# Seven half-size products for the in-projection of a conv and mLSTM layer, with one stream of split weights

## The chip, the cores and the metric

The kernel runs on one core of one Trainium2 chip. The metric is the device time of one launch in microseconds. The kernel before takes 2620.36 us (median of three runs, 2616.11 to 2622.33). Its profile is of one execution with a span of 2622.1 us. Engine names are those of the profile: PE multiplies matrices, PEld loads its weights, DVE, ACT and POOL work on vectors, SP issues the transfers.

## The reference, cut to what matters

One layer works on 2176 tokens of 1024 features: 128 context tokens, then 2048 latent ones, all through the same weights, modulated apart. Everything is fp32.

```python
h = rmsnorm(x, norm1) * (1 + scale1) + shift1
z = h @ w_in                     # 1024 x 3600: conv b, c, x; q, k, v, o; 16 gate columns
y_sc = sc_b * conv3(sc_c * sc_x)                    # short gated convolution, 512 columns
h_m, C, n, m = mlstm_bidir(q, k, v, gates, C0, n0, m0)   # chunks of 128 tokens, both directions
h_m = headnorm(h_m) * sigmoid(o)
x = x + gate1 * (concat[y_sc, h_m] @ w_out)
h2 = rmsnorm(x, norm2) * (1 + scale2) + shift2
up = conv3(h2 @ w_up)                               # 2 x 2816 columns
x = x + gate2 * ((silu(g) * a) @ w_down)
```

The scales, shifts and gates come from `silu(c) @ w_mod`, 48 tiles of 128 values for two conditionings.

## The kernel before, in words

An fp32 product is made of three: every operand is split into a high part (a copy that is rounded to fp32r) and a low part (the difference), and high x high, high x low and low x high are summed in PSUM. A split costs a copy on ACT (`wh`, `hH`) and a subtraction on POOL or DVE (`wl`, `hL`).

Tokens are taken in six blocks: five of 384 and one of 256. The second half (blocks 3 to 5, list `BB`) comes first, then the first half (`BA`). `load_w` fetches a weight tile of 1024x128, copies it on ACT (L105) and subtracts in two pieces of 512 on POOL (L108). `gemm` (L196 to L198) multiplies one weight tile with one token block: 24 matmuls, eight feature tiles by three products. `vg` (L333 to L335) makes v and the gates with the tokens as the stationary operand, 24 matmuls of 264 columns for every chunk of 128 tokens and each of two halves of the columns. So the 24 weight tiles other than v are each loaded twice, once for a half of the tokens.

The stages, in order: 16 modulation tiles on PE with the loads behind them (to about 41 us); the second half through `vg`, `heads` and `shortconv` (to about 430 us), beside which DVE makes the other 32 modulation tiles (`mod_dve`, 64 dot products of 1024 at L499); `vg` of the first half and the rows of the gates (to 477 us); `Sums`, 34 units that go backwards over the chunks (about 490 to 690 us), and `Mix`, 34 units that make the outputs (to about 1015 us). `weave` puts one block of `gemm` between two stages of these units (`fill`: q, o, the conv and the out-projection of the first half, and blocks 2 and 3). The rest of the out-projection ends at 1106 us. Then the up projection (L938 to L940) from 1114 us and the down projection (L1030 to L1032) from 2066 us.

The up projection already uses seven half-size products in place of eight (Strassen-Winograd): weights in quarters, four extra additions on DVE for a pair of tiles (L269), seven splits (ACT at L275, subtractions at L276: three on POOL, four on DVE), and sums of tokens that are made once and stored (`sums`, L229 to L235).

Every engine works through its own list in program order, and waits at the head of the list for semaphores. SP issues almost all transfers in program order.

Of the kernel before, what the change touches and what calls it, by code (L numbers as in the profile page):

```python
# [18 lines left out]
P = 128  # L19
D = 1024  # L20
KT = 8
# [3 lines left out]
H = 4  # L25
# [9 lines left out]
BA = (0, 1, 2)  # L35
BB = (3, 4, 5)
# [6 lines left out]
def chunks(b):  # L43
    t0, n = BL[b]
    return range(t0 // P, (t0 + n) // P)
# [8 lines left out]
def hymba_kernel(ctx: ExitStack, tc: tile.TileContext, I, O):  # L54
# [17 lines left out]
    uD = dr.tile([FT, P, T], F32, name="uD")  # L72

# [20 lines left out]
    ssp = ctx.enter_context(tc.tile_pool(name="ssp", bufs=2))  # L94

# [4 lines left out]

    def load_w(src, n=1024):
        st = wp.tile([P, WN], F32, name="wst", bufs=2)
        Q.dma_start(st[:, :n], src)
        wh = wp.tile([P, WN], F32R, name="wh")
        S.activation(wh[:, :n], st[:, :n], AF.Copy)  # L105
        wl = wp.tile([P, WN], F32R, name="wl")
        for a in (0, n // 2):
            G.tensor_sub(wl[:, a:a + n // 2], st[:, a:a + n // 2], wh[:, a:a + n // 2].bitcast(F32))  # L108
        return wh, wl
# [18 lines left out]
    def spread(r, n):  # L128
        """PSUM [P, n]: the columns of r along the free dimension, on every partition."""
# [6 lines left out]
    def load_x(b, src, pool, name, bufs):  # L136
        t0, n = BL[b]
        xt = []
        for kh in range(2):
            x = pool.tile([P, 4, 384], F32, name=name, bufs=bufs)  # L140
            Q.dma_start(x[:, :, :n], src[4 * kh:4 * kh + 4, :, t0:t0 + n].rearrange("k p t -> p k t"))
            xt.append(x)
        return xt

    def rcol(b):
        t0, n = BL[b]
        return rc[:, t0 // P:(t0 + n) // P]

    def squares(b, xt):
        n = BL[b][1]  # L150
        ss = ssp.tile([P, 384], F32, name="ss")
        for k in range(KT):
            x = xt[k // 4][:, k % 4, :n]
            if k == 0:
                S.activation(ss[:, :n], x, AF.Square)
                continue
            sq = sqp.tile([P, 384], F32, name="sq")
            S.activation(sq[:, :n], x, AF.Square)
            V.tensor_add(ss[:, :n], ss[:, :n], sq[:, :n])
        return ss  # L160

    def apply(b, xt, norm):
        t0, n = BL[b]
        rb = spread(rcol(b), n)
        hH, hL = h_pair()
        sh = 0 if norm == 0 else 24
        for k in range(KT):
            x = xt[k // 4][:, k % 4]
            for a, e, v in spans(t0, t0 + n):
                a, e = a - t0, e - t0  # L170
                V.scalar_tensor_tensor(x[:, a:e], x[:, a:e], ab[:, norm, k, v:v + 1], rb[:, a:e],
                                       op0=ALU.mult, op1=ALU.mult)
                sv = modT[:, sh + k, v:v + 1]
                if k % 2 == 0:
                    S.activation(hH[:, k, a:e], x[:, a:e], AF.Identity, bias=sv)
                    V.scalar_tensor_tensor(hL[:, k, a:e], x[:, a:e], sv, hH[:, k, a:e].bitcast(F32),
                                           op0=ALU.add, op1=ALU.subtract)
                else:
                    S.activation(x[:, a:e], x[:, a:e], AF.Identity, bias=sv)
                    S.activation(hH[:, k, a:e], x[:, a:e], AF.Copy)  # L180
                    G.tensor_sub(hL[:, k, a:e], x[:, a:e], hH[:, k, a:e].bitcast(F32))
        return hH, hL

    def h_pair():
        pool = hps[next(turn) % 3]
        return [pool.tile([P, KT, 384], F32R, name=n) for n in ("hH", "hL")]

    def make_h(b, src, norm):
        return apply(b, load_x(b, src, xp, "xt", 2), norm)

    def gemm(w, h, n):
        (wh, wl), (hH, hL) = w, h
        acc = pa.tile([P, 512], F32, name="acc")
        for k in range(KT):
            w_h, w_l = wh[:, k * P:(k + 1) * P], wl[:, k * P:(k + 1) * P]
            PE.matmul(acc[:, :n], w_h, hH[:, k, :n], start=(k == 0), stop=False)  # L196
            PE.matmul(acc[:, :n], w_h, hL[:, k, :n], start=False, stop=False)  # L197
            PE.matmul(acc[:, :n], w_l, hH[:, k, :n], start=False, stop=(k == KT - 1))  # L198
        return acc
# [60 lines left out]
    def weights(j):  # L260
        """The split weights of the seven products."""
        st = fp.tile([P, 2, 1024], F32, name="st", bufs=2)
        for m in range(2):
            Q.dma_start(st[:, m], I["w_up"][m * FT + j])
        a11, a12, a21, a22 = (st[:, m, k:k + 512] for m in range(2) for k in (0, 512))

        def add(op, a, b, name):
            t = fp.tile([P, 512], F32, name=name, bufs=1)
            op(t, a, b)  # L269
            return t  # L270

        def part(a, on_pool):
            wh = fp.tile([P, 512], F32R, name="wh", bufs=3)
            wl = fp.tile([P, 512], F32R, name="wl", bufs=3)
            S.activation(wh, a, AF.Copy)  # L275
            (G if on_pool else V).tensor_sub(wl, a, wh.bitcast(F32))  # L276
            return wh, wl

        yield part(a11, True)
        s1 = add(V.tensor_add, a21, a22, "s1")  # L280
        yield part(s1, False)
        s2 = add(V.tensor_sub, s1, a11, "s2")
        yield part(s2, False)
        s4 = add(V.tensor_sub, a12, s2, "s4")
        yield part(s4, False)
        s3 = add(V.tensor_sub, a11, a21, "s3")
        yield part(s3, False)
        yield part(a12, True)
        yield part(a22, True)

    def stages():
        """Products of all units, in order, each with its weights."""
        for hf in range(2):
            for j in range(FT):
                for i, w in enumerate(weights(j)):
                    yield hf, j, i, w

    # ---------------------------------------------------------------- mixer
    ph2 = ExitStack()
    with ExitStack() as ph1:  # L300
        wp = ph1.enter_context(tc.tile_pool(name="wp", bufs=4))
        xp = ph1.enter_context(tc.tile_pool(name="xp", bufs=2))
        pa = ph1.enter_context(tc.tile_pool(name="pa", bufs=4, space=PSUM))
        sqp = ph1.enter_context(tc.tile_pool(name="sqp", bufs=2))
        rp = ph1.enter_context(tc.tile_pool(name="rp", bufs=4))
        ph0 = ph1.enter_context(ExitStack())
        turn = count()
        hps = {i: (ph1 if i else ph0).enter_context(tc.tile_pool(name=f"hp{i}", bufs=1)) for i in (2, 1, 0)}
        rq = ph0.enter_context(tc.tile_pool(name="rq", bufs=2))
        phr = ExitStack()  # L310
        gp = phr.enter_context(tc.tile_pool(name="gp", bufs=1, side="right"))
        pm = phr.enter_context(tc.tile_pool(name="pm", bufs=1, space=PSUM))
# [5 lines left out]
        gates = gp.tile([P, NCH, 16], F32, name="gates")  # L318

        def load_vg(j):  # L320
            return [load_w(I["w_vg"][j, kk], WN) for kk in range(2)]

        def vg(blocks, hs, ws):
            for b in blocks:
                hH, hL = hs[b]
# [813 lines left out]
```

## Time and profile before

| what | value |
|---|---|
| times of the runs | 2620.36, 2622.33, 2616.11 us, median 2620.36 |
| span of the profiled execution (the page gives no other time of its own) | 2622.1 us |
| PE busy | 97% of the span |
| DVE, ACT, POOL busy | 57%, 41%, 27% |
| moved by DMA | 403.25 MB, 154 GB/s over the span |
| in-projection, out-projection, v and gates | to 1106 us |
| up and down projection | from 1114 us |

A row of the view by windows gives the stretch, its length, and for each engine the busy time with the count of instructions; then the granted clock of PE, the mean busy share of the 16 DMA engines and the rate. A row of the timeline gives start, duration, engine, line, operation and tiles. A group row gives the busy time, the mean duration and the idle time ahead of it with what ended it.

### The profile page before, as it was taken

What the parts mean: (1) busy time and instruction counts of PE and PEld (TensorE: products, weight loads), DVE (VectorE), ACT (ScalarE), POOL (GpSimd) and SP (SyncE); (2) the same over time, 40 slices, a digit from 0 to 9 for tenths busy, and PEclk for the clock granted to TensorE, in tenths of its full rate; (3) what the DMA queues carried; (4) which work ended last, traced back from release to release, by engine and by line L of the source; (5) the groups of instructions that cost most, each with busy time, mean ns of one, the idle gap of its engine ahead of it and who ended that gap; (6) DMA issues with size and microseconds to landing.
All of it is one profiled execution on the core that took longest, in us unless ns stands there. A gap on an engine that the chain in (4) does not pass through costs nothing. (4 is left out here: it accounts for less than half of the span.)

```text
span 2622.1 us, 46918 instructions
## 1 busy us (share of the span) xinstructions
PE 2539.1 (97%) x18511; PEld 2519.2 (96%) x18511; DVE 1501.3 (57%) x2560; ACT 1066.1 (41%) x2028; POOL 706.4 (27%) x534
## 2 busy tenths in 40 slices
PE   8999999999988988899999999999999999999998
PEld 7999999999988988899999999999999999999998
DVE  3993242333457666797686669666666635353533
ACT  4521142322345454464454446554544523232411
POOL 2542242211333344221121112111111222232232
PEclk9999999999999999999999999999999999999999
DMA  8773142555467887854252224222222635454442
GB/s 280 250 254 101 57 140 85 155 180 155 152 195 242 253 256 235 267 195 139 84 178 91 79 79 165 83 83 82 83 83 90 234 113 184 156 179 150 149 139 77
DMA packets 223582, 403.25 MB, mean 154 GB/s; under 512 B 20722, under 2 KB 144770, under 8 KB 221698
## 3 DMA queue, kind: packets, MB, share of 16 engines
q1 hardware_dynamic: 223362, 400.25, 46.5%
q8 instruction: 145, 2.38, 0.4%
q14 instruction: 75, 0.61, 0.1%
HBM read 305.13 MB, written 95.04 MB: 153 GB/s over the span
## 5 line engine op out<-in xcount | busy, mean ns | idle before, releaser
L196 PE MATMUL acc<-hH,wh 128*128 128x384 f32 (+1 forms) x1536 | 516.4, 336 | 0.0
L198 PE MATMUL acc<-hH,wl 128*128 128x384 f32 (+1 forms) x1536 | 505.0, 329 | 0.0
L197 PE MATMUL acc<-hL,wh 128*128 128x384 f32 (+1 forms) x1536 | 504.7, 329 | 0.0
L938 PE MATMUL pa<-tH,wh 128*128 128x272 f32 x1408 | 410.1, 291 | 5.6 <-DVE raw L950 5.2
L940 PE MATMUL pa<-tH,wl 128*128 128x272 f32 x1408 | 409.3, 291 | 0.4 <-DVE wl L276 0.4
L1030 PE MATMUL d<-uh,wh 128*128 128x272 f32 x1408 | 406.0, 288 | 3.1 <-ACT raw L948 3.1
L939 PE MATMUL pa<-tL,wh 128*128 128x272 f32 x1408 | 407.1, 289 | 0.0
L1032 PE MATMUL d<-uh,wl 128*128 128x272 f32 x1408 | 406.9, 289 | 0.0
L1031 PE MATMUL d<-ul,wh 128*128 128x272 f32 x1408 | 404.4, 287 | 0.0
L276 POOL TENSOR_TENSOR wl<-st,wh 128x512 fp32r<-128x512 f32 x132 | 182.3, 1381 | 730.5 <-ACT wh L275 697.5
L108 POOL TENSOR_TENSOR wl<-wst,wh 128x512 fp32r<-128x512 f32 (+1 forms) x160 | 234.3, 1486 | 434.0 <-ACT wh L105 421.5
L196 PEld LDWEIGHTS acc<-hH,wh 128*128 128x128 f32 x1536 | 291.1, 190 | 1.5 <-issue 0.4
L197 PEld LDWEIGHTS acc<-hL,wh 128*128 128x128 f32 x1536 | 291.1, 189 | 1.0
L198 PEld LDWEIGHTS acc<-hH,wl 128*128 128x128 f32 x1536 | 290.5, 189 | 0.2 <-issue 0.2
L938 PEld LDWEIGHTS pa<-tH,wh 128*128 128x128 f32 x1408 | 266.8, 190 | 6.4 <-issue 5.7
L1030 PEld LDWEIGHTS d<-uh,wh 128*128 128x128 f32 x1408 | 266.9, 190 | 3.4 <-ACT raw L948 3.3
L939 PEld LDWEIGHTS pa<-tL,wh 128*128 128x128 f32 x1408 | 267.3, 190 | 0.0
L940 PEld LDWEIGHTS pa<-tH,wl 128*128 128x128 f32 x1408 | 266.6, 189 | 0.6 <-DVE wl L276 0.6
L1032 PEld LDWEIGHTS d<-uh,wl 128*128 128x128 f32 x1408 | 266.1, 189 | 0.1
L1031 PEld LDWEIGHTS d<-ul,wh 128*128 128x128 f32 x1408 | 265.3, 188 | 0.0
L993 POOL TENSOR_TENSOR wl<-st,wh 128x704 fp32r<-128x704 f32 x64 | 150.5, 2352 | 367.2 <-ACT wh L991 358.2
L884 DVE SCALAR_TENSOR_TENSOR tt<-raw,fw,tt 128x127 f32<-128x127 f32 (+4 forms) x264 | 245.7, 959 | 1.5 <-ACT tt L890 0.8
(215 smaller groups left out, 5031.6 us busy)
## 6 DMA issues: line engine op xcount, KB each, us to landing
st<-in_w_up SPq DMA_DIRECT2D x88, 512.0 KB, 4.4
st<-in_w_down SPq DMA_DIRECT2D x64, 704.0 KB, 4.2
wst<-in_w_in SPq DMA_DIRECT2D x48, 512.0 KB, 4.1
us<-uD SPq DMA_DIRECT2D x88, 272.0 KB, 4.4
R<-nD SPq DMA_DIRECT2D x34, 512.0 KB, 5.5
wm<-in_w_modr SPq DMA_DIRECT2D x32, 512.0 KB, 4.7
F<-tD SPq DMA_DIRECT2D x12, 1088.0 KB, 8.8
uD<-tt SPq DMA_DIRECT2D x22, 576.0 KB, 2.8
```

Of the source, the lines that this page charges most:

```text
L108: G.tensor_sub(wl[:, a:a + n // 2], st[:, a:a + n // 2], wh[:, a:a + n // 2].bitcast(F32))
L196: PE.matmul(acc[:, :n], w_h, hH[:, k, :n], start=(k == 0), stop=False)
L197: PE.matmul(acc[:, :n], w_h, hL[:, k, :n], start=False, stop=False)
L198: PE.matmul(acc[:, :n], w_l, hH[:, k, :n], start=False, stop=(k == KT - 1))
L276: (G if on_pool else V).tensor_sub(wl, a, wh.bitcast(F32))
L884: V.scalar_tensor_tensor(o, i, w, o, op0=ALU.mult, op1=ALU.add)
L938: PE.matmul(acc, wh[:, w], rh, start=(kk == 0 and i in (0, 1, 5)), stop=False, skip_group_check=True)
L939: PE.matmul(acc, wh[:, w], rl, start=False, stop=False, skip_group_check=True)
L940: PE.matmul(acc, wl[:, w], rh, start=False, stop=(kk == 3), skip_group_check=True)
L1030: PE.matmul(acc[b][:, :NB], wh[:, c], uh[:, q], start=(j == 0), stop=False)
L1031: PE.matmul(acc[b][:, :NB], wh[:, c], ul[:, q], start=False, stop=False)
L1032: PE.matmul(acc[b][:, :NB], wl[:, c], uh[:, q], start=False, stop=(j == FT - 1))
```

## The change

**Products.** The tokens are three groups of two equal half groups: 1408 to 2175 (twice 384), 768 to 1407 (twice 320), 0 to 767 (twice 384), in this order. Weight tiles go in pairs. `pair` makes both tiles for both half groups in seven half products of 12 matmuls (`half`), 84 in place of 96. `vg` does likewise. The k heads of the first group are made directly (`first_heads`, 192 matmuls), while its sums of tokens are made.

**Tokens.** Of each group seven slots of 4 x 128 features are held split. `gsums` makes the four sums of the next group and stores all seven operands in DRAM (`mD`); `refill` loads one slot after each half product of the last conv pair and splits it, on POOL for three of the seven. Both run beside the products: `beside` steps the modulation dot products every fourth yield and the sums every fifth.

**Weights.** One generator, `stream`, makes all split weights from the first head to the end of the up projection, one part of 512 columns (528 for v and gates) for one half product, and `take` keeps three parts ahead. A pair takes seven copies on ACT, four additions on DVE, one subtraction on DVE and six on POOL (`MX`). The in-projection's weights are now read three times.

**Around it.** Accumulators are three and three banks, later two and one beside four for the mLSTM. `Mix.second` works on each head by itself, in a bank of its own. `weave` takes a pattern: blocks of half products between units are 1,1,1,1,1,0 in `Sums` and 2,3,2,3,2 in `Mix`. The out-projection uses `half` as well (all its subtractions on POOL). `mod_dve` writes its unused product to SBUF. The last statistics come behind the second half product of the up projection's first unit.

```diff
+GR = ((1408, 384), (768, 320), (0, 384))
...
+    def part(a, on_pool):
+        n = a.shape[-1]
+        wh = fp.tile([P, WP], F32R, name="wh", bufs=3)
+        wl = fp.tile([P, WP], F32R, name="wl", bufs=3)
+        S.activation(wh[:, :n], a, AF.Copy)
+        (G if on_pool else V).tensor_sub(wl[:, :n], a, wh[:, :n].bitcast(F32))
+        return wh, wl
...
+        yield part(a11, pool[0])
+        s1 = add(V.tensor_add, a21, a22)
+        yield part(s1, pool[1])
+        s2 = add(V.tensor_sub, s1, a11)
+        yield part(s2, pool[2])
+        s4 = add(V.tensor_sub, a12, s2)
+        yield part(s4, pool[3])
+        V.tensor_sub(a21, a11, a21)
+        yield part(a21, pool[4])
+        yield part(a12, pool[5])
+        yield part(a22, pool[6])
...
+        MX = (1, 1, 0, 1, 1, 1, 1)
+        UP = (1, 0, 0, 0, 0, 1, 1)
...
+        rest = [(12, 13), (14, 15), (20, 21), (22, 23), (4, 8), (5, 9), (0, 1), (6, 10), (7, 11), (2, 3)]
+        vgs = ([lambda: load_st_vg(0), lambda: load_st_vg(1)], unit_vg(MX))
+        units = [([pair_in(16, 17), pair_in(18, 19)], unit_heads), vgs]
+        units += [([pair_in(*p)], unit_pair(MX)) for p in rest]
+        for _ in range(2):
+            units.append(vgs)
+            units += [([pair_in(*p)], unit_pair(MX)) for p in [(16, 17), (18, 19)] + rest]
...
+        def put(s, x, n, on_pool=False):
+            S.activation(s[0][:, :, :n], x, AF.Copy)
+            (G if on_pool else V).tensor_sub(s[1][:, :, :n], x, s[0][:, :, :n].bitcast(F32))
...
+                x = fq.tile([P, 7 * 384], F32, name="F", bufs=2)[:, :4 * n].rearrange("p (k t) -> p k t", t=n)
+                Q.dma_start(x, mD[g, i][:, :, :n])
+                gs[i] = new_slot(i)
+                put(gs[i], x, n, i in (1, 2, 3))
...
+                half(acc, take(), gs[ORDER[i]], n, i in (0, 1, 5), True)
...
+            for _ in products:
+                i = next(tick)
+                if i % 4 == 0:
+                    next(md, None)
+                if i % 5 == 2:
+                    next(side, None)
+
+        side = chain(first_stats(((768, 384), (1152, 256))), gsums(1))
+        beside(chain(vg(0), heads(0, qD, None, QS), heads(0, oD, AF.Sigmoid)), side)
+        conv0 = shortconv(0, refill(1))
...
-        weave([Sums(c, hp) for c in range(NL - 1, -2, -1) for hp in range(2)], fill, 0)
-        weave([Mix(c, hp) for c in range(-1, NL) for hp in range(2)], fill, 3)
...
+            weave([Sums(c, hp) for c in range(NL - 1, -2, -1) for hp in range(2)], fill, (1, 1, 1, 1, 1, 0))
...
+        weave([Mix(c, hp) for c in range(-1, NL) for hp in range(2)], fill, (2, 3, 2, 3, 2))
```

The order of DVE's list shows what stands between the weight additions. Before, in the second half of the tokens, DVE's list beside the gemm blocks (`y,mt<-wm,cB` is a dot product of the modulation, `ss<-ss,sq` a sum of squares):

```order
L499 SCALAR_TENSOR_TENSOR y,mt<-wm,cB 128x1024 [waits DVE_49]
L340 TENSOR_TENSOR gates<-acc,bgate 128x8 [waits Activation_49]
L159 TENSOR_TENSOR ss<-ss,sq 128x384 [waits DVE_49]
L501 TENSOR_SCALAR modT<-mt,bmod 128x2 [waits DVE_49]
L499 SCALAR_TENSOR_TENSOR y,mt<-wm,cB 128x1024 [waits DMAHW0_49]
```

Now, in the first group, behind the weights of v and the gates (`s` and `st` are the weight sums, `wl` the low part that DVE makes, `jk,mt<-wm,cB` the dot product):

```order
L172 TENSOR_TENSOR s<-st 128x512 [waits DMAHW1_49,DVE_49]
L182 TENSOR_TENSOR st<-st 128x512 [waits DMAHW7_49,DMAHW0_49,DVE_49]
L165 TENSOR_TENSOR wl<-s,wh 128x528 [waits Activation_49]
L172 TENSOR_TENSOR s<-s,st 128x512 [waits DVE_49]
L716 SCALAR_TENSOR_TENSOR jk,mt<-wm,cB 128x1024 [waits DMAHW3_49,Activation_49]
L133 TENSOR_TENSOR ss<-ss,sq 128x384 [waits Activation_49]
L716 SCALAR_TENSOR_TENSOR jk,mt<-wm,cB 128x1024 [waits DVE_49]
L133 TENSOR_TENSOR ss<-ss,sq 128x384 [waits DVE_49,Activation_49]
L717 TENSOR_SCALAR modT<-mt,bmod 128x2 [waits DVE_49]
L133 TENSOR_TENSOR ss<-ss,sq 128x384 [waits DVE_49,Activation_49]
L716 SCALAR_TENSOR_TENSOR jk,mt<-wm,cB 128x1024
L172 TENSOR_TENSOR s<-st,s 128x512 [waits Pool_49]
```

The dot products and the sums of squares, which used to stand on DVE's list without any weights behind them, now stand ahead of the last weight sum of a pair (`s<-st,s`).

POOL's list before, in the second half of the tokens: two pieces for each weight tile, and the small fills of `vg`:

```order
L108 TENSOR_TENSOR wl<-wst,wh 128x512 [waits DMAHW0_49,Activation_49]
L108 TENSOR_TENSOR wl<-wst,wh 128x512
L337 MEMSET rv 128x2 [waits DMAHW4_49,Pool_49]
L108 TENSOR_TENSOR wl<-wst,wh 128x512 [waits PE_49,Activation_49]
L108 TENSOR_TENSOR wl<-wst,wh 128x512
```

Now, at the end of the first group, where the slots are filled again (`sL<-F,sH` is the low part of a slot of tokens of the next group):

```order
L165 TENSOR_TENSOR wl<-s,wh 128x512 [waits DVE_49,PE_49,Activation_49]
L165 TENSOR_TENSOR wl<-st,wh 128x512 [waits DMAHW6_49,PE_49,Activation_49]
L165 TENSOR_TENSOR wl<-st,wh 128x512 [waits PE_49,Activation_49] x2
L360 TENSOR_TENSOR sL<-F,sH 128x4x320 [waits DMAHW4_49,Activation_49]
L165 TENSOR_TENSOR wl<-st,wh 128x528 [waits DMAHW6_49,PE_49,Activation_49]
L165 TENSOR_TENSOR wl<-st,wh 128x528 [waits DMAHW2_49,PE_49,Activation_49]
L165 TENSOR_TENSOR wl<-s,wh 128x528 [waits PE_49,Activation_49]
L360 TENSOR_TENSOR sL<-F,sH 128x4x320 [waits DMAHW0_49,Activation_49]
```

POOL's subtractions each wait for a copy of ACT and, through the three buffers, for the product of PE that used the buffer; a slot of tokens with its own transfer now stands between them.

More of the change, by code (lines that the diff above doesn't have):

```diff
@@ L162, in apply @@
[L162 to L199, printed above, removed]
@@ new lines, in half @@
+    def half(acc, w, s, n, first, last):
+        (wh, wl), (sh, sl) = w, s
+        for kk in range(4):
+            c = slice(kk * P, (kk + 1) * P)
+            PE.matmul(acc, wh[:, c], sh[:, kk, :n], start=first and kk == 0, stop=False, skip_group_check=True)
+            PE.matmul(acc, wh[:, c], sl[:, kk, :n], start=False, stop=False, skip_group_check=True)
+            PE.matmul(acc, wl[:, c], sh[:, kk, :n], start=False, stop=last and kk == 3, skip_group_check=True)
+    ORDER = (6, 0, 1, 5, 2, 4, 3)
@@ new lines, in unit_pair, with parts, unit_vg, unit_heads @@
+    def unit_pair(pool):
+        def parts(sts, more):
+            yield from seven(*quarters(sts[0], 512), pool)
+        return parts
+    def unit_vg(pool):
+        def parts(sts, more):
+            a, b = (seven(*quarters(st, WP), pool) for st in sts)
+            for _ in range(7):
+                yield next(a)
+                yield next(b)
+        return parts
+    def unit_heads(sts, more):
+        for blk in range(2):
+            for kh in range(2):
+                for m in range(4):
+                    if (blk, kh, m) == (1, 1, 2):
+                        more()
+                    yield part(sts[m // 2][:, m % 2, kh * 512:(kh + 1) * 512], m % 2 == 0)
@@ L208, in sums, with take @@
+    weights = stream()
+    feed = []
+    def take():
+        while len(feed) < 3:
+            w = next(weights, None)
+            if w is None:
+                break
+            feed.append(w)
+        return feed.pop(0)
     def sums(hf, pool, pairs=range(2), direct=()):
@@ new lines, in pair @@
+        def pair(g, emit, scale=1.0, after=None):
+            t0, n = GR[g]
+            bank, cp = {}, {}
+            for i in range(7):
+                kind = KIND[i]
+                if i in (0, 1, 5):
+                    bank[kind] = pab[kind != "a"].tile([P, 512], F32, name="a" if kind == "a" else "b")
+                acc = bank[kind][:, :n]
+                half(acc, take(), gs[ORDER[i]], n, i in (0, 1, 5), True)
+                if i < 3:
+                    cp[i] = row()[:, :n]
+                    S.activation(cp[i], acc, AF.Copy, scale=scale)
+                else:
+                    m, blk, other = PLACE[i]
+                    emit(m, blk, acc, cp.get(other))
+                if after:
+                    after(i)
+                yield
```

720 lines of the change are left out of this document (431 added, 289 removed).

## The prediction

> **What bounds the kernel now.** I read the page's totals first, then the windows by stage, then the timelines of single stages.
>
> ```profile
> PE 2539.1 (97%) x18511; PEld 2519.2 (96%) x18511; DVE 1501.3 (57%) x2560; ACT 1066.1 (41%) x2028; POOL 706.4 (27%) x534
> ```
>
> PE is busy for 97% of 2622.1 us, so PE sets the time nearly everywhere, and work taken from PE is worth its full time as long as nothing else fills the place. The windows show where PE is not full:
>
> ```profile
> core 0: us, PE busy (x) PEld busy (x) DVE busy (x) ACT busy (x) POOL busy (x), PEclk, DMA share, GB/s
> 0.00:41.00 41.00, 33.14 (x272) 32.93 (x273) 16.46 (x46) 15.39 (x25) 11.15 (x18) 1.00 0.88 313
> 41.00:100.00 59.00, 53.94 (x417) 52.72 (x416) 41.85 (x86) 35.64 (x78) 22.81 (x31) 0.97 0.74 237
> 100.00:430.00 330.00, 327.40 (x2192) 326.89 (x2191) 160.40 (x281) 89.61 (x164) 111.35 (x95) 0.99 0.44 142
> 430.00:490.00 60.00, 59.24 (x334) 56.42 (x333) 22.64 (x69) 19.82 (x42) 13.58 (x11) 0.97 0.38 120
> 490.00:690.00 200.00, 199.43 (x1134) 194.12 (x1133) 63.39 (x118) 53.66 (x122) 36.75 (x26) 1.00 0.54 162
> 690.00:860.00 170.00, 152.34 (x970) 150.49 (x969) 101.83 (x263) 84.54 (x256) 62.94 (x55) 0.97 0.68 210
> 860.00:1015.00 155.00, 138.96 (x893) 137.24 (x892) 99.17 (x256) 79.67 (x240) 61.35 (x54) 0.96 0.80 250
> 1015.00:1114.00 99.00, 89.66 (x573) 88.42 (x573) 69.76 (x125) 42.73 (x85) 34.09 (x28) 0.96 0.79 259
> ```
>
> In the mixer PE has spare time in `Mix` (690 to 1015 us: 33.7 us idle, and a clock of 0.96 to 0.97, some 11 us more) and around it, almost none in the products of the second half (100 to 430 us) or in `Sums`. In these, DVE and POOL together are busy for 272 of 330 us and 100 of 200 us.
>
> **The saving on PE.** A busy duration of a matmul overlaps the next one; what counts is the distance of starts.
>
> ```profile
> 291.77 0.34 PE L196 MATMUL acc<-hH,wh 128*128 128x384 f32 x1
> ...
> 296.33 0.33 PE L198 MATMUL acc<-hH,wl 128*128 128x384 f32 x1
> ```
> ```profile
> 65.06 0.28 PE L333 MATMUL acc<-wh,hH 128*128 128x264 f32 x1
> ...
> 66.28 0.28 PE L334 MATMUL acc<-wl,hH 128*128 128x264 f32 x1
> ```
>
> There are 26 steps from the first to the last of the one, 0.175 us for 384 columns, and ten in the other, 0.122 us for 264. On the line between them 320 columns take 0.147 and 256 take 0.118 (estimates). Before: 24 tiles x 24 matmuls x (5 x 0.175 + 0.118) = 572 us. After: 192 direct ones and 10 pairs of 84 at 0.175 (181 us), 12 pairs at 0.147 (148 us), 12 pairs at 0.175 (176 us): 505 us. v and gates: 756 in place of 816 at 0.122, 7 us less. Together **-74 us**. I expect no cost for the shape of the half products, groups of 12 matmuls on one bank: the distance of starts within a group is the same.
>
> **What the split weights cost.** A tile used to be split once for three blocks of tokens. Now a pair for two half groups takes seven copies, six subtractions on POOL, one on DVE and four additions on DVE. The durations:
>
> ```profile
> L108 POOL TENSOR_TENSOR wl<-wst,wh x160: 1259/1301/2383, 22.0 to 1083.2; 128x512 fp32r<-128x512 f32 x144, 128x528 fp32r<-128x528 f32 x16
> L269 DVE TENSOR_TENSOR s<-s,st 128x512 f32<-128x512 f32 x44 | 30.1, 685 | 0.0
> L499 DVE SCALAR_TENSOR_TENSOR y<-wm,cB x64: 1219/1232/2320, 75.8 to 201.3; 128x1024 f32<-128x1024 f32 x64
> ```
>
> For a pair: POOL 6 x 1.30 = 7.8 us, DVE 5 x 0.69 = 3.4 us (its subtraction taken like an addition of the same size), beside 84 x 0.175 = 14.7 us of PE. ACT's seven copies replace those that it made before and have room (89.61 of 330 us). Each engine alone has time. But POOL and DVE do not run independently. This is the stretch before in which both work, DVE first, then POOL:
>
> ```profile
> 89.90 0.22 DVE L501 TENSOR_SCALAR modT<-mt,bmod 128x2 f32<-128x2 f32 x1
> ...
> 92.83 1.23 DVE L499 SCALAR_TENSOR_TENSOR y<-wm,cB 128x1024 f32<-128x1024 f32 x1
> ...
> 96.72 1.25 DVE L499 SCALAR_TENSOR_TENSOR y<-wm,cB 128x1024 f32<-128x1024 f32 x1
> ...
> 98.06 2.13 DVE L499 SCALAR_TENSOR_TENSOR y<-wm,cB 128x1024 f32<-128x1024 f32 x1
> ...
> 100.28 1.12 DVE L501 TENSOR_SCALAR modT<-mt,bmod 128x2 f32<-128x2 f32 x1
> ```
> ```profile
> 92.90 3.88 POOL L108 TENSOR_TENSOR wl<-wst,wh 128x512 fp32r<-128x512 f32 x2 [0.59 <-ACT wh L105]
> ...
> 96.78 4.56 POOL L108 TENSOR_TENSOR wl<-wst,wh 128x512 fp32r<-128x512 f32 x2
> ...
> 101.54 4.35 POOL L108 TENSOR_TENSOR wl<-wst,wh 128x512 fp32r<-128x512 f32 x2 [0.16 <-ACT wh L105]
> ```
>
> Two subtractions of POOL, 2.6 us by their median, take 4.56 us, and a dot product that starts beside one takes 2.13 in place of 1.23. From 96.78 to 101.54 us, 4.76 us, there are two subtractions (2.60), two dot products (2.46) and one small one (0.22): 5.28 us of work, 1.11 times the time. So I count both engines' work as one queue with a **rate of 1.11**. Work of DVE whose operand is in PSUM does not stretch in this way:
>
> ```profile
> L721 DVE SCALAR_TENSOR_TENSOR sb<-sb,decB,y 128x129 f32<-128x129 f32 x60 | 18.1, 341 | 0.0
> L779 DVE SCALAR_TENSOR_TENSOR sf<-sf,decB,sb 128x129 f32<-128x129 f32 x60 | 29.6, 527 | 0.3 <-PE y L773 0.3
> ```
>
> The same form takes 341 ns with `y` in PSUM and 527 with all in SBUF; I leave PSUM work out of the queue.
>
> The Trainium skill (SBUF — State Buffer, section "SBUF: two separate sides") goes further: a DVE operation with two SBUF inputs and a POOL operation that reads SBUF share a port pair as an exclusive lock, and the second blocks for the whole of the first. By that the rate would be 1.00 and the sum of the next part 50 us more; the rows above agree that one stretches by the other, and their 1.11 decides, as starts and ends of instructions seem to overlap.
>
> First group (v, gates and ten pairs). DVE: 64 dot products at 1.22, 78 us (all of them stand on its list before the second group's v); 48 weight additions and 13 subtractions at 0.69, 42 us; sums of squares, token sums, conv taps and refills, some 65 of 0.5 to 1.5 us, 42 us. POOL: 72 parts, 94 us; four token sums and three refills of 4 x 320 (2.5 times a subtraction, 3.2 us), 14 us. Together 270 us, at 1.11 **243 us beside 178 us of PE: +65**. The dot products did not hurt before, as DVE held nothing that PE waited for:
>
> ```profile
> 75.80:202.00 126.20, 126.20 (x848) 126.20 (x847) 121.69 (x200) 38.58 (x75) 59.05 (x40) 1.00 0.75 245
> ```
>
> They filled DVE for those 126 us while PE did not lose any. Now the last weight sum of a pair stands behind them on the same list, and three parts ahead are 6 us of cover.
>
> Second group: 70 weight additions and subtractions (48 us), the rest 45 us, POOL 84 parts and refills 126 us: 219 us, at 1.11 **197 beside 179: +18**. Bounds of both together: 0, if POOL and DVE lose nothing, and +132 at rate 1.00. I take +83; the row it is nearest to is the one with both engines busy. In later stages the same count stays below the time of PE (in `Sums` some 63 of 108 us, in `Mix` 223 of 278), so nothing there.
>
> **The other terms.** Where the second half's products stood, 41 to 430 us, 7.7 us of idle time and clocks of 0.97 and 0.99 (5 us) go with them: **-13**. The start: the second half group's x, 1.5 MB, comes behind the first, 5 us at 313 GB/s: **+5** (0 to 12). The rows of the gates had 50 us of k heads around them and now have 29; their window has 0.8 us idle: **+4** (0 to 11). `Sums` shrinks from 200 us to 38 steps of one half product (2.1 us) or none and a unit's own matmuls, 108 us of PE by my count, and carries nearly the same transfers, some 27 MB, at 256 GB/s. The row nearest to that is 1015 to 1114 us, 259 GB/s with 9% idle: **+10** (0 to 20). `Mix` is 34 units with 91 half products of 2.1 us, 278 us of PE in place of 291.
>
> ```profile
> L773 PE MATMUL y<-sf,qs 128*128 128x129 f32 x128 | 27.8, 301 | 33.3 <-DVE hv L791 33.3
> L754 POOL TENSOR_TENSOR R<-R,maskN 128x512 f32<-128x512 f32 x31 | 42.2, 1360 | 102.1 <-DMA R<-nD 100.1 <-PE st L803 1.9
> DMA packets 63330, 74.49 MB, mean 229 GB/s; under 512 B 4791, under 2 KB 53063, under 8 KB 63300
> ```
>
> Its 33.3 us of waits are for PSUM's `y`, which DVE has not yet read; a bank for each head takes these away. But POOL also waits 100 us for `R` there, and now six subtractions of every pair stand behind that wait on its list. Nearly the same bytes (78 MB by my count, with weights of a third reading) have 14% less time. I take the old 45 us of losses as staying: **0** (-34 to +35). The end of the mixer has 9.3 us idle before the up projection; parts made ahead take some: **-4** (-8 to +4).
>
> Sum against the profiled span of 2622.1, 0.07% above the median: 2622 - 74 - 13 + 5 + 83 + 4 + 10 + 0 - 4 = **2633 us**.
>
> **Rivals.** *The parts slip through* (faster): what the dot products take, POOL gets back between them. A pair alone needs 11.2 us of the common queue, 10.1 at 1.11, of its 14.7; only 4.6 are left for 8 us of dot products and other work, but if PSUM results set DVE's pace and leave gaps that POOL fills, most of the 83 goes. With 20 of it left: 2570. For it speaks the window above, where both were busy and PE lost nothing; against it, that PE needed no more than two subtractions for 12.6 us of products there. *No overlap at all*: rate 1.00 makes +132, 2682. For it the 2.13 us of a dot product, against it the 4.76 us. *Transfers hold `Mix`*: at the 229 GB/s of before, 78 MB take 341 us, 63 us over PE's 278 in place of the 45: with the clock that falls with idle time and `Sums` at its own upper bound some +35, 2668. It decides from about 240 GB/s downwards; the windows of before reach 250 and 259, which speaks against it.
>
> **How the numbers follow.** Forecast 0.45 (2612 to 2665), parts slip through 0.37, no overlap 0.08, transfers hold `Mix` 0.10. The range of 8 in 10 is 2562 to 2682: it leaves out the lower part of the second case and the end of the third. A difference of 0.2%, 5 us, is about what can be told from none. Faster: 0.35 of the second case and 0.03 of the forecast's lower end, 0.38. Same: 0.08 and 0.02, 0.10. Slower: 0.34 of the forecast and 0.18 of the other two, 0.52.
>
> **What would show it.** PE's first two groups should last about 243 and 197 us, with PE's idle time ended by `wl` (POOL or DVE) and POOL's mean subtraction near 2 us there; 178 and 179 with a mean near 1.4 would prove the first rival. `Sums` should be near 118 us, `Mix` near 325 with waits for POOL's `wl` in place of those for `hv`; 345 and more would be the transfers. The forecast is wrong if the mixer ends before about 1100 us.

## The result, and the profile after

The changed kernel takes 2737.28 us (median of four runs, 2729.02 to 2740.82), the kernel before 2620.03: **slower**, ratio 1.0441 with a 95% interval of 1.042 to 1.0462. The forecast had the direction and a ninth of the size (+13 us of +117); the time lies 55 us above the range. The page of the changed kernel, its totals:

```profile
PE 2533.8 (93%) x18045; PEld 2488.8 (91%) x18045; DVE 1842.7 (67%) x3022; ACT 1226.4 (45%) x2364; POOL 948.7 (35%) x668
```

The windows, cut at the stages of the changed kernel (columns as before): start, first group, second group, v of the third group with the gate rows, `Sums`, `Mix`, the rest of the mixer, the up projection, the down projection.

```profile
0.00:102.00 102.00, 77.61 (x471) 74.54 (x472) 61.09 (x84) 45.12 (x81) 37.09 (x30) 0.89 0.55 192
102.00:356.00 254.00, 202.45 (x1115) 196.71 (x1114) 235.18 (x356) 98.06 (x184) 135.16 (x89) 0.91 0.56 185
356.00:577.00 221.00, 196.22 (x1287) 190.90 (x1286) 174.97 (x233) 111.99 (x215) 146.04 (x107) 0.94 0.55 181
577.00:659.00 82.00, 69.90 (x444) 66.23 (x443) 55.32 (x114) 36.54 (x64) 44.61 (x36) 0.93 0.40 131
659.00:779.00 120.00, 115.55 (x616) 106.51 (x615) 75.07 (x153) 58.69 (x170) 35.85 (x27) 0.96 0.75 228
779.00:1114.00 335.00, 290.11 (x1779) 278.67 (x1779) 246.84 (x645) 178.97 (x534) 154.67 (x128) 0.94 0.74 232
1114.00:1224.00 110.00, 98.61 (x600) 97.02 (x599) 73.17 (x128) 51.55 (x99) 43.61 (x32) 0.94 0.81 270
1224.00:2179.00 955.00, 940.06 (x7427) 938.83 (x7428) 684.26 (x983) 490.56 (x837) 192.47 (x143) 0.99 0.31 108
2179.00:2739.00 560.00, 543.26 (x4320) 539.43 (x4320) 236.85 (x333) 154.93 (x182) 159.22 (x79) 0.99 0.45 151
```

The mixer ends 110 us later, at 1224 instead of 1114 us; up and down projection take 1515 us in place of 1508. Against the prediction's own sum, stage by stage ("all on DVE" is run `f2_mx_none`, "unread" is `h1_idle_pool`, both below):

| stage | forecast | changed kernel | all on DVE | unread |
|---|---|---|---|---|
| start, direct k heads | 80 | 102 | 99 | 102 |
| first group | 243 | 254 | 191 | 244 |
| second group | 197 | 221 | 210 | 267 |
| v of the third group, gate rows | 67 | 82 | 74 | 89 |
| `Sums` | 118 | 120 | 114 | 120 |
| `Mix` | 323 | 335 | 325 | 332 |
| rest of the mixer | 97 | 110 | 108 | 110 |

The two groups, `Sums` and `Mix` are forecasts that the prediction states; 80, 67 and 97 are its sum shared out over the other stages afterwards. The stages miss it by 99 us together. The up and down projection add 7 us (5 and 9 with all low parts on DVE and in run `g3_none_c`) for which the prediction had no term; the cause of these was not looked for.

In the first group PE waits at the first matmul of a half product, for accumulators (PSUM banks) that DVE frees late (groups of PE in that window):

```profile
L147 PE MATMUL a<-sH,wh 128*128 128x384 f32 x160 | 62.5, 390 | 43.7 <-DVE modT L717 12.3 <-DVE row L521 11.1 <-DVE row L488 8.0
L148 PE MATMUL a<-sL,wh 128*128 128x384 f32 x159 | 60.1, 378 | 0.0
```

Of PE's 51.5 us of idle time there 39 end with an instruction of DVE at such an accumulator, and 1.1 with a low part of POOL. DVE's timeline ahead of one of these waits, the 5.27 us that end at 229.11:

```profile
226.30 2.19 DVE L716 SCALAR_TENSOR_TENSOR jk<-wm,cB 128x1024 f32<-128x1024 f32 x1
...
228.42 0.55 DVE L486 TENSOR_TENSOR row<-a,row 128x384 f32<-128x384 f32 x1
228.89 0.21 DVE L717 TENSOR_SCALAR modT<-mt,bmod 128x2 f32<-128x2 f32 x1
```

The instruction that reads the accumulator, `row<-a,row`, stands behind stretched dot products; the profile names its neighbour `modT`, which ended last.

DVE is busy for 235 of 254 us, and with it POOL for 135. The timelines of DVE and then POOL show why this is not work but waiting:

```profile
196.67 1.25 DVE L717 TENSOR_SCALAR modT<-mt,bmod 128x2 f32<-128x2 f32 x1
197.84 1.21 DVE L716 SCALAR_TENSOR_TENSOR jk<-wm,cB 128x1024 f32<-128x1024 f32 x1
...
199.09 2.18 DVE L716 SCALAR_TENSOR_TENSOR jk<-wm,cB 128x1024 f32<-128x1024 f32 x1
...
203.05 2.21 DVE L716 SCALAR_TENSOR_TENSOR jk<-wm,cB 128x1024 f32<-128x1024 f32 x1
```
```profile
193.88 4.02 POOL L165 TENSOR_TENSOR wl<-st,wh 128x512 fp32r<-128x512 f32 x2 [0.69 <-ACT wh L164]
198.08 2.11 POOL L165 TENSOR_TENSOR wl<-st,wh 128x512 fp32r<-128x512 f32 x1 [0.18 <-ACT wh L164]
202.90 1.27 POOL L165 TENSOR_TENSOR wl<-st,wh 128x512 fp32r<-128x512 f32 x1 [2.71 <-ACT wh L164]
```

The subtraction at 198.08 takes 2.11 us because the dot product of 197.84 runs until 199.05; the next dot product, issued at 199.09, takes 2.18 because the subtraction has the turn until 200.19. The one that starts first runs at its own speed (1.21, 1.27), the other waits. Even a piece of work on two columns (196.67) takes 1.25 us behind POOL.

The long waits cost a second time. After the wait of 5.27 us the matmuls of 384 columns start 0.32 us apart in place of 0.175:

```profile
229.11 0.66 PE L147 MATMUL a<-sH,wh 128*128 128x384 f32 x1 [5.27 <-DVE modT L717]
229.57 0.52 PE L148 MATMUL a<-sL,wh 128*128 128x384 f32 x1
229.89 0.52 PE L149 MATMUL a<-sH,wl 128*128 128x384 f32 x1
```

Such slow stretches, most of them 3 to 5 us long, stand behind nine of the eleven waits of 2 us and more in the first group. From the distances of starts they cost 15 us there and some 45 us in the whole mixer (before: 8 us), an estimate. They go with the granted clock of 0.89 to 0.96 in the mixer's windows.

### The profile page after: what moved, and what is told of

It is laid out like the page before. It is cut to its first block, busy times and chain, and to the rows that moved or that the text cites. A ratio compares the mean times of both kernels' runs of the same rounds, so it can differ in the third digit from the quotient of the medians.

```text
span 2739.0 us, 47410 instructions
## 1 busy us (share of the span) xinstructions
PE 2533.8 (93%) x18045; PEld 2488.8 (91%) x18045; DVE 1842.7 (67%) x3022; ACT 1226.4 (45%) x2364; POOL 948.7 (35%) x668
## 5 line engine op out<-in xcount | busy, mean ns | idle before, releaser
L165 POOL TENSOR_TENSOR wl<-st,wh 128x512 fp32r<-128x512 f32 (+1 forms) x348 | 516.3, 1488 | 956.2 <-ACT wh L164 880.9
L164 ACT ACTIVATE wh<-st 128x512 fp32r<-128x512 f32 (+1 forms) x400 | 251.1, 629 | 371.2 <-PE pa L1168 118.3
L147 PE MATMUL a<-sH,wh 128*128 128x384 f32 (+2 forms) x832 | 296.2, 357 | 81.0 <-ACT row L469 16.7
L148 PE MATMUL a<-sL,wh 128*128 128x384 f32 (+2 forms) x832 | 286.5, 345 | 1.9 <-DVE sL L557 1.8
L149 PE MATMUL a<-sH,wl 128*128 128x384 f32 (+2 forms) x832 | 286.2, 344 | 1.7 <-POOL wl L165 1.7
L164 ACT ACTIVATE wh<-s 128x512 fp32r<-128x512 f32 (+1 forms) x252 | 158.4, 630 | 264.8 <-PE pc L1168 98.3
L147 PEld LDWEIGHTS a<-sH,wh 128*128 128x128 f32 x832 | 167.6, 202 | 93.2 <-issue 32.2
L1223 ACT ACTIVATE wh<-st 128x1408 fp32r<-128x1408 f32 x64 | 88.3, 1379 | 359.1 <-PE d L1263 222.4
```

Of the source, the lines that this page charges most:

```text
L147: PE.matmul(acc, wh[:, c], sh[:, kk, :n], start=first and kk == 0, stop=False, skip_group_check=True)
L148: PE.matmul(acc, wh[:, c], sl[:, kk, :n], start=False, stop=False, skip_group_check=True)
L149: PE.matmul(acc, wl[:, c], sh[:, kk, :n], start=False, stop=last and kk == 3, skip_group_check=True)
L164: S.activation(wh[:, :n], a, AF.Copy)
L165: (G if on_pool else V).tensor_sub(wl[:, :n], a, wh[:, :n].bitcast(F32))
```

## The experiments

**Is it the common queue of DVE and POOL, or DVE's list?** Two edits of the dot products, one that shortens them and one that leaves them as long but reads one operand from PSUM.

```diff
-                    V.scalar_tensor_tensor(jk, st, 1.0, cB[:, v], ...)
+                    V.scalar_tensor_tensor(jk[:, :64], st[:, :64], 1.0, cB[:, v, :64], ...)
```

> The 64 modulation dot products beside the first group take 64 columns in place of 1024 (their values are then not the layer's; the rest is unchanged). This takes some 70 us off DVE and off the common queue of DVE and POOL in the first group. Common port and DVE's own list both expect the first group to fall from 258 us to 185 to 200 us and the whole to about 2670 to 2680. If the waits come from the chain of products and PSUM copies itself, the first group stays above 235 us and the whole above 2715.

Measured: 2696.51 us, first group 214 us, second 218. The gain of 41 us is nearly all in the first group. It is smaller than both explanations expected, and does not tell them apart.

```diff
-                    V.scalar_tensor_tensor(jk, st, 1.0, cB[:, v], ...)
+                    V.scalar_tensor_tensor(jk.rearrange(...), st.rearrange(...), 1.0, bc(cP[:, None, :], [P, 2, 512]), ...)
```

`cP` is a PSUM bank with 512 of the values; the rearranged operands are two rows of 512.

> The same 64 dot products with the same length on DVE, but their second operand is read from a PSUM bank (512 values twice, so the modulation they give is not the layer's). DVE's list is as long as before, the port is free of them. Common port: POOL's subtractions in the first group fall from about 1.6 us to near 1.3 us, the dot products no longer stretch, the first group falls to 200 to 220 us and the whole to about 2690. DVE's own list: first group 245 to 258 us, whole 2720 to 2737.

Measured: 2695.84 us, first group 220 us. DVE has dot products of the same length to make, and yet the gain is that of shortening them to 64 columns. The line of the dot products, in the changed kernel and then with the operand in PSUM:

```profile
L716 DVE SCALAR_TENSOR_TENSOR jk<-wm,cB x64: 1207/1218/3477, 113.7 to 354.1; 128x1024 f32<-128x1024 f32 x64
```
```profile
L720 DVE SCALAR_TENSOR_TENSOR jk<-wm,cP x64: 1203/1208/1222, 116.9 to 335.3; 128x1024 f32<-128x1024 f32 x64
```

With both operands in SBUF the longest of 64 takes 3.48 us and 21 take over 1.5; with one in PSUM the longest takes 1.22, though POOL makes the same subtractions beside them. These get faster too; POOL's groups in the first group, as changed and with PSUM:

```profile
L165 POOL TENSOR_TENSOR wl<-st,wh 128x512 fp32r<-128x512 f32 (+1 forms) x46 | 85.6, 1874 | 19.4 <-ACT wh L164 18.4 <-DVE s L172 0.8
```
```profile
L165 POOL TENSOR_TENSOR wl<-st,wh 128x512 fp32r<-128x512 f32 (+1 forms) x48 | 72.6, 1521 | 25.2 <-ACT wh L164 23.4 <-PE b L149 1.6
```

1.87 us become 1.52, not 1.3, as DVE's weight sums still meet them. So what costs is the way of the operands, not the length of DVE's list alone. The Trainium skill (SBUF — State Buffer, section "Who interferes with whom") names the same pair: a DVE instruction with two SBUF inputs contends with a POOL instruction that reads SBUF, one with at most one SBUF input (outside DVE's two-port modes) does not. The 1222 and 3477 ns agree.

**Spreading the dot products.**

```diff
-                if i % 4 == 0:
+                if i % 9 == 0:
                     next(md, None)
```

> The modulation dot products come every ninth yield in place of every fourth, so that half of them move into the second group. Common port or DVE's list: the first group falls by about 30 us and the second rises by 20 to 30, the whole stays within 15 us of 2737, with fewer long waits of PE and so fewer half-clock windows (some 10 us). Chain of products: no change in either group.

Measured: 2734.31 us, both groups as they were (256 and 214 us). This is the number that the chain of products expected, but the edit did not do what it was for: the last dot product starts at 352.3 us, in the changed kernel at 354.1. Every ninth of the first group's 84 steps would leave 20 of the 64 dot products in it; all 64 are there. So the builder does not lay out an engine's list in the order of the program, as was said ahead of the prediction; by what rule it does is not shown. Inconclusive on the cause.

**Which engine makes the low parts.** First three of seven on POOL, then none.

```diff
-        MX = (1, 1, 0, 1, 1, 1, 1)
+        MX = (0, 1, 0, 1, 0, 1, 0)
```

> Of a pair's seven low parts of weights DVE makes four and POOL three (before one and six) in all three groups. Common port: three subtractions of 1.30 us become three of 0.69, some 1.8 us less of the queue for each of 34 pairs and of 6 half pairs of v and gates, 40 to 60 us faster (2680 to 2700). DVE's own list: 2 us more on DVE for a pair, the first group gets slower, 2745 to 2790.

Measured: 2692.05 us, first group 215 us, as the common port expected. More work on DVE, the busiest engine of the first group, made the kernel 45 us faster.

```diff
-        MX = (1, 1, 0, 1, 1, 1, 1)
+        MX = (0, 0, 0, 0, 0, 0, 0)
```

> DVE makes all seven low parts of a pair of the in-projection, POOL none; the values are right. Common port: the queue gets shorter still (34 x 3 x 0.6 = 62 us less than with three on POOL), but DVE's own work in the first group, some 230 us with PSUM reads, is then longer than PE's 178: the first group 225 to 245 us, the second 205 to 220, Mix some 10 us shorter than 326 since nothing on POOL's list stands behind the wait for R. The whole 2685 to 2710. A POOL that is late by itself: 2650.

Measured: 2637.78 us, **100 us less than the changed kernel**. DVE is as good as always busy, and PE waits for 7 us in the first group, where its own count was 178 us:

```profile
99.00:290.00 191.00, 183.75 (x1103) 180.07 (x1102) 186.17 (x369) 97.73 (x183) 12.05 (x18) 0.98 0.66 222
290.00:500.00 210.00, 195.53 (x1299) 190.84 (x1298) 196.11 (x377) 113.81 (x217) 28.94 (x22) 0.96 0.63 212
...
L716 DVE SCALAR_TENSOR_TENSOR jk<-wm,cB x64: 1204/1212/1226, 110.8 to 394.4; 128x1024 f32<-128x1024 f32 x64
```

My own bound by DVE's list, 225 to 245 us, was wrong: the dot products moved out into the second group (the last at 394.4 us), so DVE's work of the first group need not fit into it: 42 of the 64 are in it, where the changed kernel had all. No dot product stretches any more (1.23 us at most). The whole is nearer to the 2650 of a POOL that is merely late than to what the common port expected; the run with the unread subtractions settles that.

**Both edits together.** Three of seven low parts on POOL and the operand in PSUM.

> Both edits that each took about 42 us off: DVE makes four of a pair's seven low parts, and the 64 dot products read their second operand from PSUM (their values are not the layer's). If both take from one queue that is longer than PE's work only in the first group, they add up only as far as PE's own 178 us there: the first group about 200 us, the second 205 to 215, the whole 2665 to 2680. If they were two separate causes, the gains add up in full: about 2650.

Measured: 2669.07 us, first group 207, second 215, near what one queue expected. The two gains of 41 and 45 us give 68 together. They share a part of what they take away, as the common queue expects.

**The same load on POOL, with nobody waiting for it.** This run separates a POOL that is late from a POOL that is in the way. DVE makes all seven low parts; POOL makes six more subtractions for each pair (a 2 in `MX`) into a tile that nothing reads.

```diff
+        if on_pool == 2:
+            x = fp.tile([P, WP], F32, name="nobody", bufs=1)
+            G.tensor_sub(x[:, :n], wh[:, :n].bitcast(F32), wh[:, :n].bitcast(F32))
```

> As in the run where DVE makes all seven low parts of a pair (first group 191 us, whole 2638), but POOL also makes six subtractions of the same size for each pair, into a tile that nobody reads. PE waits for none of them. Common port: the same work on both engines stretches each other again although nothing depends on POOL; DVE now carries 78 + 42 + 48 + 30 us and POOL 94, the first group rises to 235 to 275 us, the second to 215 to 235, the whole to 2690 to 2760. If POOL's subtractions cost by being late for PE, nothing changes: first group 188 to 196, whole 2630 to 2645.

Measured: 2782.52 us, 145 us more than without these subtractions. First group 244 us, second 267; the second group and the whole are even longer than the common port expected. The groups' windows, and the subtractions:

```profile
102.00:346.00 244.00, 200.60 (x1102) 190.51 (x1100) 239.86 (x370) 97.34 (x183) 113.65 (x89) 0.93 0.53 175
346.00:613.00 267.00, 216.11 (x1302) 203.90 (x1302) 260.26 (x375) 115.69 (x218) 153.63 (x107) 0.91 0.50 167
...
L168 POOL TENSOR_TENSOR nobody<-wh 128x512 f32<-128x512 f32 x204 | 291.8, 1430 | 317.4 <-ACT wh L164 313.1
```

Of what waits for them, the view of waits from 102 to 613 us has one line: ACT's next copy into the buffer they read, 8.7 us in nine times.

```profile
ACT wh L164 <- POOL nobody L168: 8.7, 9, 1.5
```

So the loss comes by way of DVE, whose busy time grows by 54 us in the first group's window and by 64 in the second's without any added work. The order of DVE's list is not the difference: both runs have 42 of the 64 dot products in the first group, at 1214 ns each without and 1457 ns with the unread subtractions.

**Mix, the tail and the start.** Five of seven low parts on DVE, and the out-projection's low parts alternating (`kh == 0` on POOL, else DVE):

> DVE makes five of a pair's seven low parts, POOL two, and the out-projection's low parts alternate between DVE and POOL (before all on POOL); the values are right. Common port: first group 215 to 225 us, second 210 to 220, Mix and the tail together 5 to 15 us shorter than with three of seven on POOL (436), the whole 2675 to 2690. If Mix and the tail do not depend on POOL's list, the whole stays at 2690 to 2700.

Measured: 2647.66 us, 27 us less than the least that was expected; the first group takes 202 us, the second 215. `Mix` and the rest of the mixer take 422 us (445 as changed, 436 with three of seven on POOL, 433 with none and the out-projection on POOL). So POOL cost there as well, though the prediction's count of both engines' work in `Mix`, 223 us, lay below PE's 278.

All seven on DVE, the first group's direct k heads all on POOL, the out-projection alternating:

> DVE makes all low parts of the in-projection's pairs; POOL makes all of the first group's direct k heads; the out-projection's low parts alternate between POOL and DVE. Values are right. If POOL's subtractions cost by the common queue wherever they meet DVE, and the weights of the first heads wait for DVE's long token sums, the start falls from 99 us to 90 to 95, Mix and the tail together from 433 to 415 to 425, the whole to 2610 to 2625. If the first heads wait for the tokens themselves and Mix for its transfers, the whole stays at 2630 to 2640.

Measured: 2628.90 us, between the two expectations. The start stays at 101 us, so the split of the heads' weights on DVE is not what holds it. `Mix` and the rest are 428 us, by the rest alone (101 in place of 108).

The same with the token rows loaded one step earlier:

```diff
+                    xr = []
+                    for k in range(k0, k0 + 4):
+                        xr.append(row()[:, :w])
+                        Q.dma_start(xr[-1], I["x"][k][:, b0:b0 + w])
+                    yield
```

> The same, and the token rows for the next group's statistics are loaded one step of the side work before ACT squares them. If ACT's list, with a square at its head that waits for its transfer, holds the copies of products and weights behind it, the second group falls from 210 us by 4 to 8 us, and its waits of PE for copies of ACT go with it; the whole 5 to 8 us below the run without this edit. If these waits come from the weight sums alone, no difference.

Measured: 2637.26 us, 8 us more. The second group fell by 5 us, as expected (205 to 200), but the first rose by 6 and v with the gate rows by 8; why is not shown, the builder may have laid the lists out anew. The wait it aimed at is real in the run that it was read from (`f2_mx_none`, ACT's timeline, where PE waits 3.14 us for the copy of 357.66):

```profile
354.61 0.52 ACT L129 ACTIVATE ss<-row 128x384 f32<-128x384 f32 x1 [2.45 <-DMA row<-in_x]
356.50 0.52 ACT L132 ACTIVATE sq<-row 128x384 f32<-128x384 f32 x1 [1.37 <-DMA row<-in_x]
...
357.66 0.62 ACT L164 ACTIVATE wh<-s 128x512 fp32r<-128x512 f32 x1
```

No gain of it in the time was shown.

All low parts of in- and out-projection on DVE:

> DVE makes all low parts of the in-projection's pairs and of the out-projection; the first heads as in the change. If POOL's list (the wait for R in Mix) and its port cost Mix and the tail, they fall below the 415 to 425 us that the alternating split should give; if DVE's list is the longer one there, they rise to 430 and more.

Measured: 2624.94 us, ratio to the kernel before 1.0017 (1.0002 to 1.0032). This is the lowest time of the change, though its runs overlap with those of the alternating split, and it still does not beat the kernel before. `Mix` and the rest are 426 us, against 428 with the alternating split: neither expectation came true, and whether DVE makes half or all of the out-projection's low parts makes no difference that shows (the 422 us with two of seven on POOL lie lower still). The mixer ends at 1111 us, 3 us earlier than before the change. Of the 74 us that PE was to save, the start (100 us, forecast 80) and the second group (205 us, beside 179 of PE's own work) alone take 46 back.

**One part of the change in the kernel before.** A PSUM bank for each head and the restructured second step of `Mix`, with three accumulators for the projections.

> The kernel before with one part of the change alone: each head of the mLSTM has a PSUM bank of its own (three of one bank in place of one of two), its outputs are worked out head by head, and the projections have three accumulators in place of four. If the 33 us of waits for PSUM in Mix go away without a new wait, Mix falls from 325 us to about 295 and the whole to 2585 to 2595. If the transfers of Mix or the wait for R take their place, the whole stays at 2605 to 2620.

Measured: 2618.33 us beside 2618.47, no difference (0.999 to 1.0009). PE's waits for `hv` went from 33.3 to 17.1 us:

```profile
L780 PE MATMUL y<-sf,qs 128*128 128x129 f32 x128 | 27.6, 300 | 17.3 <-DVE hv L790 17.1
```

In the two traces `Mix`, from its first product to its last `hv`, takes 324 us in place of 331. New waits of some 7 us stand beside the old ones, the granted clock was 0.98 in its first half and 0.94 in the second (before 0.97 and 0.96), and the mixer's earlier stages lost 3 us, with one wait of 3.5 us for an accumulator among them. So taking half of the 33 us of waits for PSUM away from `Mix` was worth a few us at most.

## Why the prediction was right or wrong

**What bounds the kernel; the saving on PE.** Right as a count of PE's work: with POOL out of the way the first group takes 191 us, 7 of them idle, and the prediction's own count was 178. The half products cost next to nothing by their shape. What it was to be worth was lost, as other things filled the place: no run of the change is faster than the kernel before.

**The common queue.** That POOL and DVE hold each other up was right, and the first group's own number near (243 forecast, 254 measured), POOL's subtractions at 1.87 and 1.62 us in the mean near the 2 us that were to show it. The runs bear out both sides: the same dot products no longer stretch with an operand in PSUM, and unread subtractions cost 145 us. The path from there to PE was another than forecast: PE was to wait for low parts (`wl`) behind a late weight sum, but in the first group it waited for accumulators, 39 of 51.5 us, since DVE's reading of them stands on the same list. The prediction left work on PSUM out of its queue and had no term for the 15 us of slow matmuls, so that the first group's nearness is in part luck. The step that failed is the rule that I made from the queue: that the queue costs only where its work is longer than PE's, "nothing there" for the later stages. Taking POOL's low parts away gave 63 us in the first group, but also 11 in the second, 8 in v and the gate rows, 6 in `Sums` and 10 in `Mix`. Where an instruction meets one of the other engine, it is late by up to the whole of that one (POOL by a whole chain of DVE's, as the last section shows), and what is held ready for PE (three parts of weights, the free accumulators) does not always cover it, though both engines have idle time in the mean. The second group, +18 forecast, has +42, the term that was mis-sized most.

**The clock.** The other step that failed, a term that was missing. The -13 counted slow stretches of the clock as going away, and none as coming. The runs of waits that the common queue makes, 2 to 6 us long, brought a loss of 15 us by slow matmuls in the first group and of some 45 us in the mixer. I had noted the 0.96 of `Mix` and did not carry it to the groups in which I forecast as much waiting.

**The start.** +5 forecast, +27 measured. Reading the bytes was not enough: the transfers are at 55% there, and after its first matmul PE waits 19 us, at the tokens' splits (3.9 and 2.8 us, on ACT), the low parts of the first weights (7.7 us, on DVE), a power on POOL (2.8 us) and the modulation tiles (1.7 us), the last of which now end at 51 us. The start stays at 98 to 105 us in all runs. Which of its chains sets it was not settled; moving the heads' low parts to POOL did not help.

**Gate rows, `Sums`, `Mix`, the rest.** `Sums` was right in its number (118 and 120), by luck in part: 6 us of it go with POOL's low parts, for which it had no term. v and the gate rows missed by 15, `Mix` by 12, the rest by 13 us. In `Mix` the waits for `hv` went as forecast, from 33.3 to 2.1 us, but PE is idle for 45 us all the same, and low parts of POOL end only 0.9 us of that. The two largest of the new waits:

```profile
PE S L985 <- DMA q<-qD: 10.5, 4, 4.6
PE a L147 <- ACT row L469: 9.1, 7, 2.9
```

Of the 25 us that `Mix` and the rest are over the forecast together, 12 go with the in-projection's low parts on POOL (445 to 433 us) and another 7 with the out-projection's (433 to 426). These are differences of single profiled executions. The remainder, some 6 us, stays open.

**The rivals.** "The parts slip through" is ruled out in the changed kernel. "No overlap at all" at 2682 had its mechanism nearly right: two instructions do exclude each other, and the 1.11 comes from their ends. In the rows above, the subtraction of 198.08 and the dot product of 199.09 end 1.14 and 1.08 us after what they waited for, and take 1.27 and 1.21 alone: 2.48 us of work in 2.22, or 1.12. "Transfers hold `Mix`" is true of a part at most: at 232 GB/s PE waits 10.5 us for `q`, but with all of the in-projection's low parts on DVE `Mix` moves 238 GB/s and takes 325 us, near the forecast of 323, so the rate was not at a limit.

**The range.** Every term was taken for itself and bounded small, and they missed in the same direction, as one cause, POOL and DVE in each other's way, and its consequence, the clock, run through all stages of the mixer. A range made of single bounds does not hold that.

## What to carry to other kernels

Work on two engines that read SBUF by the same way has to be counted as one list, and waits come already before that list is longer than the critical engine's: an instruction moved to an "idle" POOL can be worth less than nothing, and moving it to the busier DVE gained 100 us here. An engine that also frees the matrix engine's accumulators holds it up by that, even when no weight is late. Before splitting such work over both, compare the longest and the median duration of the lines concerned; 1.2 and 3.5 us on one line tell of it, while the mean share of each engine does not. A stall of a few microseconds on the matrix engine has to be priced with the slow stretch behind it, and a saving that needs more side work has to be costed at the side work's worst neighbour, not in the mean.

## What was not expected of the hardware

Small work stretches as much as large: an operation on two columns took 1.25 us behind POOL's subtraction, and in the run with the unread subtractions POOL's power of three columns took 4.17 us, in place of the 0.85 us that it takes at the least. DVE ran one two-operand instruction after the other in that time:

```profile
403.75 0.67 DVE L175 TENSOR_TENSOR s<-s,st 128x512 f32<-128x512 f32 x1
...
407.57 0.69 DVE L165 TENSOR_TENSOR wl<-s,wh 128x512 fp32r<-128x512 f32 x1 [0.21 <-ACT wh L164]
```
```profile
403.90 4.17 POOL L114 TENSOR_TENSOR rc<-rc,mhalf 128x3 f32<-128x3 f32 x1 [0.59 <-DVE rc L113]
```

So POOL waits for a whole chain of DVE's instructions, not for one. The same power takes 7.13 us in the run with all low parts on DVE, beside nine such instructions of DVE, one behind the other. The longest subtraction of the changed kernel, 4.80 us against a median of 1.31, stands beside eight of them:

```profile
L165 POOL TENSOR_TENSOR wl<-st,wh x348: 1262/1309/4801, 22.0 to 2161.3; 128x512 fp32r<-128x512 f32 x162, 128x528 fp32r<-128x528 f32 x12
```
